# The order of the three passes of an output projection in a two-layer hybrid decoder trunk

## The chip, the core and the metric

The kernel runs on one core of one Trainium2 chip. The metric is the device time of one execution in microseconds (us). The kernel before takes 1791.77 us, the median of three runs (1791.28 to 1794.01). PE is TensorE, DVE is VectorE, ACT is ScalarE, POOL is GpSimd and SP is SyncE, which issues most of the loads.

## What is computed

The input is 512 tokens of width 1024 in float32. Each of the two layers is a feed-forward block, a mixer, and a second feed-forward block. The mixer has two groups of 512 channels each, and one output projection for both:

```python
x = x + 0.5 * swiglu(rms_norm(x, ffn1_norm[l]), ...)
h = rms_norm(x, mix_norm[l])
a, g, q, k, v = jnp.split(h @ w_in[l], splits, axis=-1)
conv_out = conv_module(a, g, conv_w[l], conv_b[l], conv_norm[l])
...
diff_out = diff_attention(q, k, v, rel_bias, lam, lam_init, subln_norm[l])
x = x + jnp.concatenate([conv_out, diff_out], axis=-1) @ w_out[l]
x = x + 0.5 * swiglu(rms_norm(x, ffn2_norm[l]), ...)
```

The conv group is a gated linear unit, a causal depthwise convolution of 31 taps, an RMS norm over the channels and a swish. The attention group is causal: for each of 4 heads, two softmax maps over the same values, of which one is taken from the other with a factor; queries are swept in 4 blocks of 128.

## The kernel before

**Layout.** Activations lie with features on the partitions: `x` is 8 tiles of 128 features by 512 tokens. Every product that matters is made in three matmuls (`mm3`, lines 199, 202, 203): both operands are split into a rounded part and a remainder (`whi`, `wlo` for weights; `acth`, `actl` for activations), and hi by hi, hi by lo and lo by hi are summed in PSUM.

**Weights.** `chunk` (lines 104 to 110) loads 128 rows by 1024 columns in two pieces of 512 columns on SP's queue (line 108) into `wraw`, and `parts_of` splits each: ACT copies it to `whi` (line 100), and DVE or POOL takes the difference to `wlo` (line 101). For the output projection the difference is made by POOL (the argument `G`). These tiles come from rings: 5 buffers of `wraw`, 9 of `whi` and 9 of `wlo`. A buffer is filled again when its last reader is done. One piece of the output weights serves one column block of 128 outputs (`wpart`): 4 tiles of the contraction by 128 columns.

**Order of the work.** The program is written as one stream. A scheduler sorts it at compile time into a fixed queue for each engine: it simulates the time at which each instruction becomes ready and, among the ready ones, prefers those written earlier. At run time each engine works its queue in order and waits on semaphores. Some instructions are held in program order by hand (in the feed-forward blocks); those of the output projection are not.

**The mixer** (`mixer`). After the input projections, `attend` (line 972 on) runs 16 steps, query block 3 first and block 0 last, four heads each. A step makes two score matmuls (line 908) into banks of the tags "sc" and "po", adds the bias and takes a minimum on DVE (line 912), the exponential on ACT (line 916), combines the two maps on DVE (line 922), transposes the map (line 929, copy by ACT in line 931) and multiplies with the values (line 938). After the fourth head of a block, its output is normed (lines 945 to 953), transposed (line 965) and split into `acth` and `actl`, feature tiles 4 to 7, for its 128 tokens (lines 967 and 968). The convolution's taps run on DVE (line 877) and POOL beside it; `conv_finish` then norms the four channel tiles (line 888 on POOL), takes the swish (line 890 on ACT, line 891 on DVE) and writes the split result to `acth` and `actl`, feature tiles 0 to 3 (lines 892 on ACT and 893 on DVE).

**The output projection** is the last part of the mixer. It goes over three pairs of a group and a range of tokens: the conv group (`half` 0) for all 512 tokens, then the attention group (`half` 1) for tokens 256 to 511, then the attention group for tokens 0 to 255. Each pass makes 8 column blocks of 12 matmuls into banks that alternate between the tags "sc" and "po" (two banks each), and DVE adds each block to `x` (line 1016). The list `w` holds the split weights; it is emptied at the start of the first two passes, so the third uses the tiles of the second. In the third pass, and behind it, `after` prepares the next feed-forward block's input (lines 291 to 300) for each finished tile of `x`.

**Behind it** comes the second feed-forward block (`begin`, `ffn`), whose first weights use the same rings and the same SP queue.

Of the kernel before, what the change touches and what calls it, by code (L numbers as in the profile page):

```python
# [20 lines left out]
SEQ = 512  # L21
# [48 lines left out]
def trunk(ctx: ExitStack, tc: tile.TileContext, xt, par, lamv, relb, onehot,  # L70
# [17 lines left out]
    def bank(tag, name):  # L88
        return psum.tile([P, 512], F32, tag=tag, name=name, bufs=BANKS[tag])
# [14 lines left out]
    def chunk(src, eng=None):  # L104
        w = []
        for n in range(2):
            raw = ring("wraw")
            nc.sync.dma_start(raw, src[:, n * 512 : (n + 1) * 512])
            w.append(parts_of(raw, eng))
        return w  # L110

    def wpart(w, b, n=P):
        hi, lo = w[b * n // 512]
        c = b * n % 512
        return hi[:, c : c + n], lo[:, c : c + n]
# [81 lines left out]
    def mm3(ps, w, x, start, stop, pin=False):  # L197
        (wh, wl), (xh, xl) = w, x
        first = T.matmul(ps, wh, xh, start=start, stop=False)  # L199
        if pin:  # L200
            tc.keep_in_program_order(first)
        T.matmul(ps, wh, xl, start=False, stop=False)  # L202
        T.matmul(ps, wl, xh, start=False, stop=stop)  # L203
# [532 lines left out]
    def mixer(l, pr, after, begun):  # L736
        with tc.tile_pool(name="mix", bufs=1) as mp, tc.tile_pool(name="mt", bufs=2) as mt:
# [265 lines left out]

            for half, t in ((0, slice(0, SEQ)), (1, slice(SEQ // 2, SEQ)), (1, slice(0, SEQ // 2))):
                if t.stop == SEQ:
                    w = [None] * 4
                for m in range(KT):
                    if w[m // 2] is None:  # L1010
                        w[m // 2] = chunk(wout[l, half, m // 2], G)
                    ps = bank(("sc", "po")[m % 2], "ps_out")[:, : t.stop - t.start]
                    for kk in range(4):
                        k = half * 4 + kk
                        mm3(ps, wpart(w[m // 2], (m % 2) * 4 + kk), (ch[:, k, t], cl[:, k, t]), kk == 0, kk == 3)
                    V.tensor_tensor(x[:, m, t], ps, x[:, m, t], op=ALU.add)

                    if half == 1 and t.start == 0 and m < KT // 2:
                        after(m)
# [14 lines left out]
    for l in range(DEPTH):  # L1034
        nxt = {}

        def preparing(gain, l2=l):
            def after(m):
                if m == 0:
                    nxt["p"] = Prep(l2, gain)  # L1040
                nxt["p"].tile(m)
            return after

        def store(m):
            nc.sync.dma_start(out[m], x[:, m, :])

        with tc.tile_pool(name="ffn", bufs=1) as fp:
            begun = ffn(fp, pr, gu1[l], dn1[l], preparing("mix_norm"), begun,
                        lambda tail: begin(nxt["p"], [[wag[l, c, i] for i in range(2)] for c in range(2)], tail),
                        (l == 0, 1), aside if l == 0 else None)  # L1050
        mixer(l, nxt["p"], preparing("ffn2_norm"), begun)
        with tc.tile_pool(name="ffn", bufs=1) as fp:
            begun = begin(nxt["p"], [[gu2[l, m, i] for i in range(2)] for m in range(2)])
            if l + 1 < DEPTH:
                begun = ffn(fp, nxt["p"], gu2[l], dn2[l], preparing("ffn1_norm", l + 1), begun,
                            lambda tail: begin(nxt["p"], [[gu1[l + 1, m, i] for i in range(2)] for m in range(2)], tail), (0, 1))
            else:
                ffn(fp, nxt["p"], gu2[l], dn2[l], store, begun, lambda tail: tail(), (0, 0))
        pr = nxt["p"]
# [74 lines left out]
```

## Time and profile before

| | |
|---|---|
| median of three runs | 1791.77 us |
| the profiled execution | 1792.68 us |
| its span, first to last instruction | 1790.9 us |
| mean granted clock of PE | 0.995 |
| output projection, layer 0: first and last matmul start | 506.22 and 554.78 us |
| output projection, layer 1: first and last matmul start | 1394.26 and 1442.32 us |
| loads of output weights | 32, of 256 KB |

A line of the timeline gives the start, the length from the first start to the last end, the engine, the line of the kernel, the operation, what it writes and reads, and the count of merged instructions. What stands in square brackets is the idle time of the engine just before, and what ended it. Matmuls overlap in the pipeline, so the spacing of their starts tells their rate, not their length. The granted clock is the share of full speed that PE's clock was given.

### The profile page before, as it was taken

The numbers are of one execution on the slowest core, as the hardware profiler recorded it, in microseconds if no ns is written. First come the engines' busy times: TensorE is split into PE (matmuls) and PEld (weight loads), VectorE is DVE, ScalarE is ACT, GpSimd is POOL, SyncE is SP. The second block draws the span as 40 slices with busy tenths as digits, with TensorE's granted clock in tenths as the row PEclk, the third lists the DMA queues.
The fourth block names the chain that finished last, engine by engine and source line by source line (L and its number), as shares of the span: only waits on it lengthen the run. The fifth ranks groups of instructions, "written<-read, shape, count | busy, mean of one in ns | idle before, by whom it ended". The sixth has DMA issues, their size and how long they took to land.

```text
span 1790.9 us, 32884 instructions
## 1 busy us (share of the span) xinstructions
PE 1767.7 (99%) x11844; PEld 1623.8 (91%) x11844; DVE 1475.3 (82%) x2595; ACT 1028.0 (57%) x1930; POOL 555.0 (31%) x523
## 2 busy tenths in 40 slices
PE   8999999999989999999999999999999999999998
PEld 7799999988778889999988999999887888999998
DVE  7969888968867959889987798889688488698887
ACT  5546566655844536556644565666559354465664
POOL 3011112379842011112310121123898320111121
PEclk9999999999999999999999999999999999999999
DMA  6457677533112447677543577766231134476775
GB/s 220 133 137 188 171 197 169 152 107 101 59 48 89 124 124 183 170 190 184 141 143 105 150 177 185 190 162 172 80 100 48 48 107 132 130 186 160 202 177 124
DMA packets 163012, 253.58 MB, mean 142 GB/s; under 512 B 18871, under 2 KB 60614, under 8 KB 162848
## 3 DMA queue, kind: packets, MB, share of 16 engines
q1 hardware_dynamic: 126144, 197.19, 34.2%
q0 software_dynamic: 36416, 54.12, 18.5%
q8 instruction: 93, 1.52, 0.3%
q14 instruction: 71, 0.58, 0.1%
q10 hardware_dynamic: 288, 0.16, 0.0%
HBM read 249.28 MB, written 3.42 MB: 141 GB/s over the span
## 4 chain that ended last, share of the span: by engine, by line
PE 90%; DVE 4%; ACT 4%; DMA 1%; issue 1%; POOL 1%; SPq 0%; ACTq 0%; DVEq 0%; POOLq 0%
PE ps_pair L413 36%; PE ps_pair L502 14%; PE ps_pair L202 9%; PE ps_pair L199 9%; PE ps_pair L203 9%; PE ps_out L199 2%; PE ps_out L202 2%; PE ps_out L203 2%; PE ps_pair L793 2%; PE ps_pair L792 2%; PE ps_pair L791 2%; ACT whi L100 1%; DMA wraw<-in_dn 1%; PE ps_v L821 0%; PE ps_sc L908 0%
## 5 line engine op out<-in xcount | busy, mean ns | idle before, releaser
L100 ACT ACTIVATE whi<-wraw 128x512 fp32r<-128x512 f32 x736 | 447.2, 627 | 419.0 <-PE ps_pair L202 163.1
L101 DVE TENSOR_TENSOR wlo<-wraw,whi 128x512 fp32r<-128x512 f32 x648 | 440.1, 698 | 108.8 <-ACT whi L100 93.5
L159 POOL DMA_DIRECT2D wsum<-in_gu x128 | 112.3, 914 | 708.6 <-DMA wsum<-in_gu 308.7
L413 PE MATMUL ps_pair<-acth,wlo 128*128 128x256 f32 x1024 | 289.8, 283 | 0.0
L413 PE MATMUL ps_pair<-actl,whi 128*128 128x256 f32 x1024 | 289.8, 283 | 0.0
L413 PE MATMUL ps_pair<-acth,whi 128*128 128x256 f32 x1024 | 289.8, 283 | 0.0
L413 PE MATMUL ps_pair<-th,whi 128*128 128x256 f32 x768 | 217.3, 283 | 0.0
L413 PE MATMUL ps_pair<-tl,whi 128*128 128x256 f32 x768 | 217.3, 283 | 0.0
L413 PE MATMUL ps_pair<-th,wlo 128*128 128x256 f32 x768 | 217.3, 283 | 0.0
L199 PE MATMUL ps_pair<-acth,whi 128*128 128x512 f32 x512 | 200.2, 395 | 5.6 <-ACT whi L100 5.6
L202 PE MATMUL ps_pair<-actl,whi 128*128 128x512 f32 x512 | 200.3, 392 | 0.0
L203 PE MATMUL ps_pair<-acth,wlo 128*128 128x512 f32 x512 | 199.5, 391 | 0.0
L413 PEld LDWEIGHTS ps_pair<-actl,whi 128*128 128x128 f32 x1024 | 196.6, 192 | 0.2
L413 PEld LDWEIGHTS ps_pair<-acth,whi 128*128 128x128 f32 x1024 | 196.6, 192 | 0.2
L413 PEld LDWEIGHTS ps_pair<-acth,wlo 128*128 128x128 f32 x1024 | 196.6, 192 | 0.0
L159 POOL DMA_DIRECT2D wsum<-in_dn x112 | 98.9, 1137 | 269.6 <-DVE wlo L101 49.9
L413 PEld LDWEIGHTS ps_pair<-th,whi 128*128 128x128 f32 x768 | 147.5, 192 | 0.0
L413 PEld LDWEIGHTS ps_pair<-tl,whi 128*128 128x128 f32 x768 | 147.5, 192 | 0.0
L413 PEld LDWEIGHTS ps_pair<-th,wlo 128*128 128x128 f32 x768 | 147.5, 192 | 0.0
L101 DVE TENSOR_TENSOR wlo<-wsum,whi 128x512 fp32r<-128x512 f32 x192 | 130.4, 685 | 20.2 <-ACT whi L100 16.3
L502 PE MATMUL ps_pair<-hh,whi 128*128 128x256 f32 x512 | 144.9, 283 | 0.0
L502 PE MATMUL ps_pair<-hl,whi 128*128 128x256 f32 x512 | 144.9, 283 | 0.0
(201 smaller groups left out, 4481.0 us busy)
## 6 DMA issues: line engine op xcount, KB each, us to landing
wraw<-in_gu SPq DMA_DIRECT2D x288, 256.0 KB, 3.4
wsum<-in_gu SPq DMA_DIRECT2D x128, 256.0 KB, 3.8
wsum<-in_gu POOLq DMA_DIRECT2D x128, 256.0 KB, 4.7
wraw<-in_dn SPq DMA_DIRECT2D x68, 256.0 KB, 3.1
wraw<-in_wqkv SPq DMA_DIRECT2D x48, 256.0 KB, 2.7
wraw<-in_dn SPq DMA_DIRECT2D x64, 128.0 KB, 3.3
wraw<-in_wag SPq DMA_DIRECT2D x32, 256.0 KB, 2.8
wraw<-in_wout SPq DMA_DIRECT2D x32, 256.0 KB, 2.7
```

Of the source, the lines that this page charges most:

```text
L100: S.activation(hi, raw, AF.Copy)
L101: (eng or V).tensor_tensor(out=lo, in0=raw, in1=f32(hi), op=ALU.subtract)
L159: nc.gpsimd.dma_start(dst[:, to], src, accum_op=ALU.add)
L199: first = T.matmul(ps, wh, xh, start=start, stop=False)
L202: T.matmul(ps, wh, xl, start=False, stop=False)
L203: T.matmul(ps, wl, xh, start=False, stop=stop)
L413: mm = T.matmul(ps, l, r, start=first and i == j == 0, stop=False, skip_group_check=True)
L502: mm = T.matmul(ps, s[:, f], r, start=side not in self.begun, stop=False, skip_group_check=True)
L791: T.matmul(ps[n], xh[:, t], wh, start=k == 0, stop=False)
L792: T.matmul(ps[n], xh[:, t], wl, start=False, stop=False)
L793: T.matmul(ps[n], xl[:, t], wh, start=False, stop=k == KT - 1)
```

## The change

```diff
-            for half, t in ((0, slice(0, SEQ)), (1, slice(SEQ // 2, SEQ)), (1, slice(0, SEQ // 2))):
-                if t.stop == SEQ:
-                    w = [None] * 4
+            for half, t in ((1, slice(SEQ // 2, SEQ)), (0, slice(0, SEQ)), (1, slice(0, SEQ // 2))):
+                w = [None] * 4
                 for m in range(KT):
                     if w[m // 2] is None:
                         w[m // 2] = chunk(wout[l, half, m // 2], G)
```

The attention group for tokens 256 to 511 is taken first, the conv group second, the attention group for tokens 0 to 255 third, as before. The list of weights is emptied at the start of every pass. The conv group lies between the two attention passes, so the attention weights are loaded and split twice: 24 pieces per layer where there were 16. Matmuls, their shapes, the banks' tags and the additions to `x` stay as many as they were. The weights of the first attention pass take the place of the conv weights at the head of the loads, and the conv weights follow them.

## The prediction

> **What bounds the kernel now.** I read the page first: the busy line, and the shares of the chain that ended last.
>
> ```profile
> PE 1767.7 (99%) x11844; PEld 1623.8 (91%) x11844; DVE 1475.3 (82%) x2595; ACT 1028.0 (57%) x1930; POOL 555.0 (31%) x523
> PE 90%; DVE 4%; ACT 4%; DMA 1%; issue 1%; POOL 1%; SPq 0%; ACTq 0%; DVEq 0%; POOLq 0%
> ```
>
> PE is busy for 1767.7 of 1790.9 us and makes 90% of the chain. The change leaves the matmuls as many as they are, so it can win only time in which PE idles or runs slowly. I then read PE's timeline where the output projection begins, in layer 0 and in layer 1.
>
> ```profile
> 490.16 0.60 PE L965 MATMUL ps_o<-ident,ov 128*128 128x128 f32 x4
> 490.59 0.83 PE L938 MATMUL ps_o<-vv,at 128*128 128x128 f32 x6
> ...
> 501.58 0.49 PE L908 MATMUL ps_sc<-kt,qz 128*128 128x128 f32 x2 [0.79 <-DVE e L922]
> ...
> 502.55 0.33 PE L929 MATMUL ps_at<-ident,e 128*128 128x128 f32 x1 [0.37 <-DVE mn L912]
> ...
> 503.88 0.49 PE L938 MATMUL ps_o<-vv,at 128*128 128x128 f32 x2 [0.78 <-ACT at L931]
> ...
> 506.22 2.08 PE L199 MATMUL ps_out<-acth,whi 128*128 128x512 f32 x4 [1.75 <-ACT acth L892]
> ...
> 520.53 0.39 PE L202 MATMUL ps_out<-actl,whi 128*128 128x512 f32 x1
> 520.76 0.39 PE L203 MATMUL ps_out<-acth,wlo 128*128 128x512 f32 x1
> ...
> 531.87 0.28 PE L199 MATMUL ps_out<-acth,whi 128*128 128x256 f32 x1
> ```
>
> ```profile
> 1389.62 0.49 PE L908 MATMUL ps_sc<-kt,qz 128*128 128x128 f32 x2 [0.80 <-DVE e L922]
> ...
> 1390.59 0.33 PE L929 MATMUL ps_at<-ident,e 128*128 128x128 f32 x1 [0.37 <-DVE mn L912]
> ...
> 1391.92 0.49 PE L938 MATMUL ps_o<-vv,at 128*128 128x128 f32 x2 [0.78 <-ACT at L931]
> ...
> 1392.98 0.79 PE L938 MATMUL ps_o<-vv,at 128*128 128x128 f32 x2 [0.43 <-ACT at L931]
> 1394.26 2.07 PE L199 MATMUL ps_out<-acth,whi 128*128 128x512 f32 x4 [0.48 <-ACT acth L892]
> ```
>
> The brackets are PE's idle time: 0.79 + 0.37 + 0.78 + 1.75 = 3.69 us in layer 0 and 0.80 + 0.37 + 0.78 + 0.43 + 0.48 = 2.86 us in layer 1. From one 512-wide matmul to the next it is 0.23 us (520.53 to 520.76; from 520.53 to 531.87 there are 50, 0.227 us each), and the 192 256-wide ones run from 531.87 to 554.90 (last fence of this part), 0.12 us each. Four 128-wide ones take from 490.16 to 490.59, 0.11 us each. The first matmuls of the projection are slower, and the windows say why (columns: window, its length, PE busy and instructions, granted clock, DMA share, GB/s).
>
> ```profile
> 506.22:511.83 5.61, 5.61 (x14) 0.51 0.00 0
> 1394.26:1399.38 5.12, 5.12 (x12) 0.52 0.00 0
> ```
>
> PE is busy throughout, at half the clock. In layer 0 these are twelve 512-wide and two 128-wide matmuls, at full clock 12 x 0.227 + 2 x 0.11 = 2.95 us, so 2.66 us are lost; in layer 1 5.12 - 2.73 = 2.39 us. All that can be won here is 3.69 + 2.66 = **6.35 us** and 2.86 + 2.39 = **5.25 us**, together 11.6 us.
>
> **The change part by part.** *The attention group of tokens 256 to 511 goes first* (96 matmuls, 96 x 0.12 = 11.5 us, which I call the first pass). Its operands and banks, on DVE:
>
> ```profile
> 499.13 0.28 DVE L912 CUSTOM_DVE_ANT_0 e<-ps_sc,bias 128x128 f32<-128x128 f32 x1
> ...
> 499.34 0.74 DVE L968 SCALAR_TENSOR_TENSOR actl<-ps_o,gsub,acth 128x512 fp32r<-128x512 f32 x1
> ...
> 501.94 0.35 DVE L922 SCALAR_TENSOR_TENSOR e<-ps_sc,c,e 128x128 f32<-128x128 f32 x1
> ...
> 503.86 1.56 DVE L891 SCALAR_TENSOR_TENSOR yp<-th,yp 128x512 f32<-128x512 f32 x1
> ...
> 506.87 0.68 DVE L891 SCALAR_TENSOR_TENSOR u<-th,u 128x512 f32<-128x512 f32 x1
> ...
> 512.85 0.74 DVE L893 SCALAR_TENSOR_TENSOR actl<-u,ghalf,acth 128x512 fp32r<-128x512 f32 x1
> ```
>
> L968 at 499.34 writes the split output of query block 2; block 3 came before it. So the operands stand at 500.08. The projection takes its banks from the tags "sc" and "po", which the maps still use: the last map leaves "sc" after L912 at 499.41, the one before it leaves "po" after L922 at 502.29. The first pass can start at about 500.2 with column blocks 0 and 2 (12 x 0.12 = 1.44 us each), and block 1 waits for 502.29. If PE takes strictly 0, 1, 2, it waits from about 501.9, 0.4 us. So I leave 0 to 0.4 us per layer in place, and take 0.4.
>
> Blocks 1 and 0 still write acth and actl, in stripes of the same tile between those that the pass reads. That such a write doesn't hold up the reader is seen elsewhere:
>
> ```profile
> 193.25 0.28 PE L502 MATMUL ps_pair<-yl,whi 128*128 128x256 f32 x1
> ```
>
> ```profile
> 193.44 0.95 DVE L473 TENSOR_TENSOR yl<-ht,yh 128x768 fp32r<-128x768 f32 x1
> ```
>
> PE reads other stripes of yl before DVE's write, earlier in the program, has begun.
>
> *The conv group becomes second.* Its chain (L891, L892, L893 for four channel tiles) ends at 513.59 now. PE's work from 500.2 on is 11.5 us of first pass and the rest of the attention (L908, L929, L938, L965, some 21 128-wide ones, 2.3 us); with the 0.4 us it reaches the conv group at about 514.4. DVE gets the first pass's eight additions inside the chain's stretch (groups of 515 to 545 us, then windows with PE, weight load, DVE, ACT, POOL busy and the clock):
>
> ```profile
> L101 POOL TENSOR_TENSOR wlo<-wraw,whi 128x512 fp32r<-128x512 f32 x7 | 8.9, 1294 | 10.0 <-ACT whi L100 10.0
> ...
> L1016 DVE TENSOR_TENSOR x<-ps_out,x 128x256 f32<-128x256 f32 x8 | 3.4, 425 | 7.2 <-PE ps_out L203 7.1
> ```
>
> ```profile
> 504.90:508.30 3.40, 2.08 (x5) 1.70 (x6) 2.31 (x4) 2.21 (x5) 2.92 (x2) 0.50 0.00 0
> 508.30:511.70 3.40, 3.40 (x10) 2.72 (x10) 3.21 (x6) 2.44 (x5) 1.14 (x2) 0.50 0.00 0
> ```
>
> The eight additions are 3.4 us, and DVE idles 1.09 + 0.19 = 1.28 us in these windows, so the chain ends some 2.1 us later, at 515.7. With three of four channel tiles there, PE has nine matmuls (2.0 us, to 516.4) on one column block, or 36 (8.2 us) if the queue interleaves four blocks, as it does now (x4 at 506.22). So the wait lies between nothing and 3.7 us per layer (worked out under the rivals). I take 1.0, near the lower end, for the row at 506.22.
>
> *The weights.* 24 loads per layer take the place of 16: the second attention pass loads its own again. Seven of now sixteen pieces are split after 515 (the row of POOL above), so nine early, up to the size of the ring:
>
> ```profile
> 478.63 2.51 POOL L101 TENSOR_TENSOR wlo<-wraw,whi 128x512 fp32r<-128x512 f32 x2
> ...
> 502.72 3.64 POOL L888 TENSOR_TENSOR u<-u,rb 128x512 f32<-128x512 f32 x3
> ...
> 510.76 1.45 POOL L243 TENSOR_TENSOR rs_y<-so,mhalf 128x4 f32<-128x4 f32 x1
> ```
>
> ```profile
> 520.96 0.64 ACT L100 ACTIVATE whi<-wraw 128x512 fp32r<-128x512 f32 x1 [0.28 <-PE ps_out L202]
> ```
>
> After the change the early nine are all eight of the first pass and one of the conv group. The other seven conv pieces follow as the first pass frees slots (as ACT at 520.96 waits for a matmul): one per 1.44 us, ACT 0.63, POOL 1.29 us. At worst POOL begins them at 512.2, after L243, and has them ready at 513.5 + 1.3k; the conv group needs piece k at 514.4 + 2.72k. Nothing is late, and POOL is the cover. The eight new pieces of the last pass (ACT 8 x 0.63 = 5.0, POOL 8 x 1.29 = 10.3 us per layer) are split during the conv group's 21.8 us, in which each column block frees one slot; eight of nine slots hold them when the last pass starts. Cost nothing; without that cover each would cost 1.9 us.
>
> ```profile
> 592.39 0.92 POOL L159 DMA_DIRECT2D wsum<-in_gu  x1 [23.07 <-DMA wsum<-in_gu]
> ```
>
> ```profile
> SPq L108 <- POOL wlo L101: 93.8, 24, 39.2
> ```
>
> ```profile
> wraw<-in_wout SPq DMA_DIRECT2D x32, 256.0 KB, 2.7
> ```
>
> POOL's next own transfer is issued at 592.39, long behind the added splits. The loads' queue waits for buffers (24 waits, 93.8 us from 430 to 560), not the reverse; a load lands in 2.7 us. Behind the eight added loads stand FFN2's first weights, on the same queue. Their slots come free with the last pass, as now, and their raw buffers when pieces 3 to 7 of it are split, before it starts. Cost nothing; the bound is one landing, 2.7 us per layer.
>
> *What is late next.* The last pass and FFN2 follow without a gap now, and PE waits 0.3 us in the 345 us behind:
>
> ```profile
> 554.78 0.28 PE L203 MATMUL ps_out<-acth,wlo 128*128 128x256 f32 x1
> 554.90 0.40 PE L199 MATMUL ps_pair<-acth,whi 128*128 128x512 f32 x1
> ```
>
> ```profile
> PE ps_pair L502 <- ACT keep L535: 0.3, 1, 0.3
> ```
>
> So what is won is kept. **Sum:** 11.6 - 2 x (0.4 + 1.0) = 8.8 us. The profiled execution took 1792.68 us (span 1790.9 and 1.8 around it), which gives 1783.9; it stands 0.9 above the median 1791.77, which gives **1783**.
>
> **The rivals.** *The conv chain comes late.* L891 took 1.56 us at 503.86 and 0.68 at 506.87; in the first case POOL's L888 (from 502.72) ran beside it. The POOL splits that now stand beside five of the chain's instructions could stretch each by the difference of these rows, up to 0.88 us: 4.4 us, and the chain ends at 515.7 + 4.4 = 520.1. PE then stands from 516.4 to 520.1, 3.7 us, if the blocks aren't interleaved: 11.6 - 2 x (0.4 + 3.7) = 3.4, **1788**; half the stretch gives 1.5 us, 7.8, 1784. Of the Trainium skill, the page "SBUF — State Buffer", section "Who interferes with whom", says that a DVE instruction with two SBUF inputs and a GpSimd instruction that reads SBUF exclude one another; by it this rival holds, and the pair of L891 rows agrees.
>
> *The clock falls all the same.* The longest wait was 1.75 us (0.80 in layer 1) and the clock fell in both layers. If filling the gaps doesn't hold it up, 2.66 + 2.39 us stay lost: 8.8 - 5.05 = 3.75, **1788**. The rows speak for the gaps: the clock is full in the uninterrupted matmuls behind. Of the Trainium skill, "TensorE: Matmul & The Clock Gate", section "Why this matters for your kernels", counts only PE-idle gaps of over about 3 us as bringing the slow clock; by it the drop here has another cause and would stay, and the trace's 1.75 us speaks against that figure.
>
> *The pass doesn't start early.* The order on each engine is fixed before the run; if the first pass is queued behind the last map's matmuls and L938, it starts at 506 and again at half clock: nothing won, **1792**.
>
> *Slower: the queues of ACT and DVE put the chain behind the first pass.* The splits on ACT wait for PE to free a slot, the additions on DVE wait for a matmul. If they are queued ahead of L890 to L893, the chain (503.86 to 513.59, 9.7 us) starts only when the pass ends. PE then idles 9.7 us and restarts at half clock (2.66): 12.4 against 6.35 to win, 6 us lost per layer, **1804**. It decides from the point where the last channel tile comes later than 514.4 + 6.35 = 520.7. Against it: the chain is earlier in the program, and DVE and ACT idle between its steps now.
>
> **How the numbers follow.** Forecast 1783 (own range 1780 to 1785): 0.58. Late chain, 1784 to 1788: 0.12, a quarter of it beyond the bound. Clock, 1788: 0.06, half of it beyond. No early start, 1792: 0.08. Slower, 1796 to 1804: 0.16. A measurement of this kernel can tell about 0.2%, 3.6 us, from no change: faster is below 1788.2, slower above 1795.4. Faster 0.58 + 0.09 + 0.03 = 0.70, same 0.03 + 0.03 + 0.08 = 0.14, slower 0.16. The range runs from 1779, the whole 11.6 us and one for the spread, to 1793, with the cases of no gain; it leaves out the slower case and little more.
>
> **What would show it.** First L199 on ps_out with 128x256 at about 500.2 (1388.2), and no wait over 0.5 us before the first 512-wide one at about 514; granted clock 1.00 in windows from 502 to 515; the last 128x256 ending some 4 to 5 us earlier against the start of the projection's stretch; L100 on wout 48 times. Wrong would be: waits on L892 or L893 after 514, clock 0.5 there, or the first ps_out at 506.

## The result, and the profile after

The changed kernel takes **1780.16 us**, the median of six runs (1778.98 to 1780.86), against 1791.97 (1791.28 to 1794.01, six runs) for the kernel before: a ratio of 0.9931, with a 95% interval of 0.9918 to 0.9944. The forecast was 1783, in a range of 1779 to 1793, with faster at 0.70. The profiled executions are 13.7 us apart (1792.68 and 1778.98), the medians 11.8: the one before stands 0.7 us above its median, the one after 1.2 below.

From the page after, the busy line, the chain that ended last, and the loads of output weights:

```profile
span 1777.2 us, 32962 instructions
...
PE 1760.0 (99%) x11844; PEld 1619.0 (91%) x11844; DVE 1478.7 (83%) x2595; ACT 1037.6 (58%) x1946; POOL 579.7 (33%) x539
...
PE 90%; ACT 3%; DVE 3%; DMA 2%; issue 1%; POOL 1%; SPq 0%; ACTq 0%; DVEq 0%; POOLq 0%
...
wraw<-in_wout SPq DMA_DIRECT2D x48, 256.0 KB, 2.6
```

PE has the same 11844 matmuls, and is busy 7.7 us less, although nothing was taken from it: a busy PE at half clock counts as busy (in the prediction's window from 506.22 us it is busy for all 5.61 us at 0.51), and so does the end of a matmul that nothing follows at once (see the idle time below). POOL has 24.7 us more of work (the 16 more splits) and ACT 9.6; neither shows in the time. That POOL's share rose from 31% to 33% tells nothing of whether that work lies on the path.

PE's timeline after, in layer 0, and its last line from layer 1:

```profile
498.79 0.39 PE L199 MATMUL ps_out<-acth,whi 128*128 128x256 f32 x1
...
500.92 0.36 PE L202 MATMUL ps_out<-actl,whi 128*128 128x256 f32 x1
...
503.63 0.39 PE L908 MATMUL ps_sc<-kt,qz 128*128 128x128 f32 x2
503.86 0.27 PE L929 MATMUL ps_at<-ident,e 128*128 128x128 f32 x1
503.88 0.36 PE L199 MATMUL ps_out<-acth,whi 128*128 128x256 f32 x1
...
508.59 0.51 PE L199 MATMUL ps_out<-acth,whi 128*128 128x512 f32 x2
508.94 0.28 PE L202 MATMUL ps_out<-actl,whi 128*128 128x256 f32 x1
...
547.71 0.40 PE L199 MATMUL ps_pair<-acth,whi 128*128 128x512 f32 x1
...
1428.34 0.40 PE L199 MATMUL ps_pair<-acth,whi 128*128 128x512 f32 x1
```

The short attention matmuls (L908, L929) that stood alone before, each behind an idle time, now stand between 256-wide matmuls without a bracket. At 508.59 the first 512-wide matmul of the conv group is already in the queue, between blocks of the first pass: the scheduler mixed the two passes. FFN2's first matmul starts at 547.71, where it started at 554.90, and in layer 1 at 1428.34.

PE's granted clock in four windows after (the third number from the end):

```profile
501.70:505.10 3.40, 3.40 (x31) 3.40 (x30) 2.39 (x9) 2.51 (x6) 3.40 (x4) 1.00 0.00 0
505.10:508.50 3.40, 3.40 (x31) 3.40 (x31) 3.14 (x8) 2.76 (x6) 3.40 (x3) 1.00 0.00 0
508.50:511.90 3.40, 3.40 (x30) 3.27 (x29) 3.06 (x4) 1.81 (x4) 3.40 (x4) 1.00 0.21 62
511.90:515.30 3.40, 3.40 (x27) 3.18 (x26) 2.94 (x4) 2.94 (x5) 3.40 (x3) 1.00 0.48 156
```

PE is busy through all four, at full clock, where it had 0.51 before.

**One length for all kernels below.** I measure the end of the mixer from the row sums of the conv norm (line 250, started before the stretch in question) to FFN2's first matmul. In the timeline of the kernel before, PE:

```profile
494.32 0.60 PE L250 MATMUL ps_rows<-ident,csum 128*128 128x128 f32 x4
...
1382.36 0.60 PE L250 MATMUL ps_rows<-ident,csum 128*128 128x128 f32 x4
...
1442.44 0.40 PE L199 MATMUL ps_pair<-acth,whi 128*128 128x512 f32 x1
```

and in that of the kernel after:

```profile
494.58 0.60 PE L250 MATMUL ps_rows<-ident,csum 128*128 128x128 f32 x4
...
1375.22 0.60 PE L250 MATMUL ps_rows<-ident,csum 128*128 128x128 f32 x4
```

I call this length the **step**. Before: 554.90 - 494.32 = 60.58 us in layer 0 and 1442.44 - 1382.36 = 60.08 in layer 1. After: 53.13 and 53.12. The gain is 7.45 + 6.96 = **14.4 us**. Outside the steps 0.7 us are given back (0.26 before layer 0's, 0.05 between the two, 0.4 behind layer 1's), which leaves the 13.7 of the two spans. So the whole effect lies in these two stretches.

### The profile page after: what moved, and what is told of

Read it like the earlier page. It is cut to its first block, busy times and chain, and to the rows that moved or that the text cites. A ratio compares the mean times of both kernels' runs of the same rounds, so it can differ in the third digit from the quotient of the medians.

```text
span 1777.2 us, 32962 instructions
## 1 busy us (share of the span) xinstructions
PE 1760.0 (99%) x11844; PEld 1619.0 (91%) x11844; DVE 1478.7 (83%) x2595; ACT 1037.6 (58%) x1946; POOL 579.7 (33%) x539
## 4 chain that ended last, share of the span: by engine, by line
PE 90%; ACT 3%; DVE 3%; DMA 2%; issue 1%; POOL 1%; SPq 0%; ACTq 0%; DVEq 0%; POOLq 0%
PE ps_pair L413 36%; PE ps_pair L502 14%; PE ps_pair L202 9%; PE ps_pair L203 9%; PE ps_pair L199 9%; PE ps_out L199 2%; PE ps_out L202 2%; PE ps_out L203 2%; PE ps_pair L793 2%; PE ps_pair L792 2%; PE ps_pair L791 2%; DMA wraw<-in_dn 1%; ACT whi L100 1%; PE ps_sc L908 0%; DVE actl L292 0%
## 5 line engine op out<-in xcount | busy, mean ns | idle before, releaser
L100 ACT ACTIVATE whi<-wraw 128x512 fp32r<-128x512 f32 x752 | 457.4, 627 | 406.8 <-PE ps_pair L202 160.5
L101 POOL TENSOR_TENSOR wlo<-wraw,whi 128x512 fp32r<-128x512 f32 x104 | 137.1, 1339 | 26.4 <-ACT whi L100 20.5
```

The source lines that it names most:

```text
L100: S.activation(hi, raw, AF.Copy)
L101: (eng or V).tensor_tensor(out=lo, in0=raw, in1=f32(hi), op=ALU.subtract)
```

## The experiments

**Theory A** (mine): the early pass gives PE work while the last attention blocks and the conv chain finish; that fills PE's idle time, and since PE no longer idles the clock isn't lowered. Rivals: the gain comes from the order or the second loading of the weights (**B**); the clock falls for a reason of its own; the conv chain, drawn out by POOL, takes part of the gain back. Each kernel was run beside the kernel before, whose median was 1792.89 beside the first eight and 1792.74 beside the last two.

### The second loading alone, in the old order

```diff
-            for half, t in ((1, slice(SEQ // 2, SEQ)), (0, slice(0, SEQ)), (1, slice(0, SEQ // 2))):
+            for half, t in ((0, slice(0, SEQ)), (1, slice(SEQ // 2, SEQ)), (1, slice(0, SEQ // 2))):
```

(against the changed kernel, so that `w = [None] * 4` stays)

> The old order of the passes, but the weights are loaded and split anew in every pass: 24 pieces per layer as in the changed kernel. Theory A (the gain is time in which PE stood still or ran at half clock before the conv group; the second loading is hidden): the time of before, 1792 within 2 us, granted clock 0.5 again in the 5 to 6 us behind the first ps_out matmul. Theory B (the gain comes from the buffers, which come free earlier when the weights aren't held through two passes): 1780 to 1786. If the second loading costs something that the changed kernel had to win back: 1794 to 1797.

Measured: 1792.63 us, ratio 1.0 (0.9991 to 1.0009), with 48 loads. The 8 loads, 8 ACT copies and 8 POOL splits per layer cost nothing, and win nothing: theory B falls.

### The new order in layer 0 alone

```diff
+            up, conv, low = (1, slice(SEQ // 2, SEQ)), (0, slice(0, SEQ)), (1, slice(0, SEQ // 2))
+            for half, t in (up, conv, low) if l == 0 else (conv, up, low):
+                if l == 0 or t.stop == SEQ:
                     w = [None] * 4
```

> The new order in layer 0 only. Theory A: the two layers' stretches are separate, layer 0 gives 7.4 us by the two traces (the step from the 490th us to the first FFN2 matmul), so 1784.5 to 1786 against 1792; layer 1's stretch as before, clock 0.5 there. If the gain is a better schedule of the whole program: nothing like half, 1780 or 1790.

Measured: 1786.25 us, ratio 0.9964 (0.9951 to 0.9976), 0.25 us above the expected span, beside a kernel before that took 0.9 us more here than in the runs of the result. The step is 53.13 us in layer 0 and 60.40 in layer 1: the gain is half, and belongs to the layer that is changed.

### The old order with useless matmuls in the gap

```diff
             conv_finish()
+            idle = bank("y", "ps_idle")[:, : SEQ // 2]
+            for n in range(28):
+                k = CT + n % CT
+                T.matmul(idle, ones_r, ch[:, k, SEQ // 2 :], start=n == 0, stop=n == 27)
```

The 28 matmuls go to a bank that nobody reads; the rest is the kernel before.

> The old order, and 28 matmuls per layer of 128x256 into a bank that nobody reads, in the gap before the conv group (28 x 0.12 = 3.4 us of work that serves nothing). They leave the waits for the conv chain where they are and only keep PE active. Theory A with the clock following PE's idleness: granted clock 1.00 behind the first ps_out matmul, 2.66 + 2.39 = 5.0 us less than before, 1787. Theory C (the clock falls for another reason): clock 0.5, 1792 or up to 2 us more.

Measured: 1787.84 us, ratio 0.9975 (0.9965 to 0.9984), steps of 58.20 and 58.17. This is the kernel before with more work to do, and it is faster. PE's waits from 480 to 560 us (line, what it waited for, us in total, times, longest), and its windows:

```profile
PE ps_o L938 <- ACT at L931: 0.8, 2, 0.5
PE ps_idle L1007 <- ACT rb L278: 0.6, 1, 0.6
PE ps_out L199 <- ACT acth L892: 0.3, 1, 0.3
PE ps_sc L908 <- DVE e L922: 0.3, 1, 0.3
```

```profile
501.70:505.10 3.40, 2.76 (x21) 2.55 (x21) 2.00 (x10) 1.86 (x6) 2.29 (x3) 1.00 0.02 5
505.10:508.50 3.40, 3.40 (x25) 3.13 (x24) 2.81 (x5) 2.02 (x6) 3.40 (x4) 1.00 0.00 0
508.50:511.90 3.40, 3.07 (x16) 2.36 (x15) 3.10 (x7) 1.78 (x4) 1.32 (x1) 1.00 0.00 0
511.90:515.30 3.40, 3.40 (x20) 2.83 (x19) 1.84 (x3) 2.38 (x5) 0.00 (x0) 1.00 0.00 0
```

The clock is 1.00 throughout, with the conv group, its weights and its chain where they were: the half clock followed PE's idleness and nothing else that the change touches. The useless matmuls (28 x 0.12 = 3.4 us per layer) stand roughly for the idle time that they fill (PE's waits in the stretch shown fall from 4.8 to 2.0 us), so what is left as gain is the clock: 5.05 us by the medians, 2.38 + 1.91 = 4.3 by the steps, where the prediction had 2.66 + 2.39. The rule that the prediction weighed, of the Trainium skill, "TensorE: Matmul & The Clock Gate", section "Why this matters for your kernels" (of gaps that bring the slow clock back, it names PE-idle ones of over about 3 us), does not agree as a limit: in the kernel before no gap was longer than 1.75 us in layer 0 and 0.80 us in layer 1, and the clock was halved in both.

### Only two column blocks first

```diff
+            up, conv, low = slice(SEQ // 2, SEQ), slice(0, SEQ), slice(0, SEQ // 2)
+            for half, t, ms in ((1, up, range(2)), (0, conv, range(KT)), (1, up, range(2, KT)), (1, low, range(KT))):
                 w = [None] * 4
-                for m in range(KT):
+                for m in ms:
```

> Only two of the eight column blocks of tokens 256 to 511 go first (2 x 1.44 = 2.9 us of PE work), the other six behind the conv group. Theory A: 2.9 of some 4.5 us of each layer's standing time are filled, 5.8 us in both layers; with the clock kept up 5.0 more, 1781; with the clock falling all the same, 1786. PE waits for the conv chain again (L892 or L893 as releaser), 1 to 2 us per layer. If order alone or the buffers made the gain: 1780 without such waits.

Measured: 1782.93 us, ratio 0.9951 (0.9939 to 0.9964), steps of 55.52 and 55.49, clock 1.00. A quarter of the early work (2.9 of 11.5 us) brings 5.06 of layer 0's 7.45 us. The clock is won first; what remains is idle time. The time is 2 us above the expected 1781, and the wait for the conv chain is smaller than expected, 0.2 us per layer (L893); the other waits of this stretch (2.2 us from 480 to 560 us) are for the maps of the attention.

### The blocks of the first two passes kept in program order

```diff
                         mm3(ps, wpart(w[m // 2], (m % 2) * 4 + kk), (ch[:, k, t], cl[:, k, t]), kk == 0, kk == 3,
+                            pin=t.stop == SEQ)
```

> The changed kernel, but the matmuls of the first two passes are kept in program order: column block after column block, no mixing of four blocks or of the two passes. The conv chain ends at 517.4 in the changed kernel. Theory A (the mixing of blocks hides the late chain): PE waits 0.4 us for a bank of the tag po in the first pass and about 1.0 us per layer for L892 or L893 in the conv group, 1783 (this is the sum of the prediction with its two reserves). If the mixing does nothing: 1780.

Measured: 1783.94 us, ratio 0.9958 (0.9946 to 0.997), steps of 55.58 in both layers. The changed kernel itself, run again beside it:

> The changed kernel once more, to stand beside the next three on the same chip: 1780 within 1.5 us.

Measured: 1779.33 us (five runs), ratio 0.9926 (0.9913 to 0.9939), steps of 53.12 and 53.13. PE's waits from 480 to 560 us with the blocks in order:

```profile
PE ps_o L938 <- ACT at L931: 1.3, 3, 0.5
PE ps_out L202 <- DVE actl L893: 1.0, 1, 1.0
PE ps_sc L908 <- DVE e L922: 0.3, 1, 0.3
```

and those of the changed kernel, in the same window:

```profile
PE ps_o L938 <- ACT at L931: 0.8, 2, 0.5
PE ps_sc L908 <- DVE e L922: 0.3, 1, 0.3
```

With the blocks in order PE waits 1.0 us for the conv chain's last result (L893) and 0.5 us more for the maps that stand between the blocks. Free to mix, it has neither wait: the mixing is worth 55.58 - 53.13 = 2.45 us per layer, and the late chain is real but covered. The waits make up 1.5 of the 2.45 us; the rest was not taken apart. The expected wait of 0.4 us for a bank did not come.

### The conv weights split by DVE instead of POOL

```diff
-                        w[m // 2] = chunk(wout[l, half, m // 2], G)
+                        w[m // 2] = chunk(wout[l, half, m // 2], V if half == 0 else G)
```

> The changed kernel, but the conv group's eight weight pieces are split by DVE and not by POOL. The two L891 that took 1.78 us beside POOL's splits should take 0.7 us, and the conv chain loses about 2 us of length but shares DVE with eight splits of 0.69 us. Theory A (the chain has cover): 1780 within 2 us, however the chain ends. If POOL's splits beside DVE cost time in the changed kernel: 1776 to 1778.

Measured: 1790.51 us, from 1782.93 to 1797.05 over twelve runs, ratio 0.9987 (0.9973 to 1.0). This missed by 10 us: the gain is gone. The loss begins long before the projection. DVE's, POOL's and PE's timelines in the profiled execution of this kernel:

```profile
477.25 5.33 DVE L101 TENSOR_TENSOR wlo<-wraw,whi 128x512 fp32r<-128x512 f32 x1 [0.32 <-POOL wlo L101]
```

```profile
475.86 2.51 POOL L101 TENSOR_TENSOR wlo<-wraw,whi 128x512 fp32r<-128x512 f32 x2
478.33 1.27 POOL L863 TENSOR_TENSOR yp<-yp,prod 128x512 f32<-128x512 f32 x1
479.55 1.26 POOL L101 TENSOR_TENSOR wlo<-wraw,whi 128x512 fp32r<-128x512 f32 x1
480.77 1.26 POOL L863 TENSOR_TENSOR yp<-yp,prod 128x512 f32<-128x512 f32 x1
```

```profile
484.15 2.50 PE L908 MATMUL ps_sc<-kt,qz 128*128 128x384 f32 x4 [4.23 <-DVE e L922]
```

One split, which takes DVE 0.68 us when it is alone (513.41 in the next kernel), took 5.33 us: it ends at 482.58, 0.55 us after POOL's unbroken run of five instructions (480.77 + 1.26 = 482.03). DVE's map work (L922) stands in the queue behind it, and PE idles 4.23 us for that. Behind the stop PE's clock is halved, long before the projection:

```profile
484.15:488.00 3.85, 3.85 (x12) 2.96 (x13) 2.32 (x8) 2.62 (x7) 1.27 (x1) 0.50 0.52 173
```

The steps of this kernel are 56.78 and 56.81 us, with two waits of PE for DVE in layer 0, 0.7 us (an addition) and 0.5 us (L953); what makes up the 3.7 us more than in the changed kernel, the delay ahead of them or DVE's other splits, the next kernel separates in part. The trace is that of one execution, of 1793.4 us. Over the twelve the mean granted clock goes with the time, from 1.000 in the fastest to 0.996 in the slowest; whether the stop is absent in the fast ones no trace shows.

### The same, but the first piece stays on POOL

```diff
+                        w[m // 2] = chunk(wout[l, half, m // 2], V if half == 0 and m else G)
```

> The changed order, with the conv projection's pieces split by DVE instead of POOL, except the first piece (row blocks 0 and 1), which stays on POOL. Theory S (the one DVE split at 477 us that took 5.33 us beside an unbroken run of POOL, and the 4.2 us that PE waited behind it at 484 us, are all that the version with every conv split on DVE lost): no wait of 4 us on PE ahead of the projection, steps from the row sums to the next feed-forward of about 53.1 us in both layers, 1780 us (1778 to 1782). Theory T (DVE's splits beside the conv chain cost by themselves, because they delay the scores' and the chain's own DVE work): 1784 to 1790, with PE waiting for DVE inside the projection and steps of 55 to 57 us.

Measured: **1777.95 us** (1777.85 to 1779.54), ratio 0.992 (0.9906 to 0.9933), steps of 53.17 and 53.16. Theory S holds: with the two splits of the first piece on POOL, the first DVE split of the stretch comes at 505 us, and the eleven from there to 547 us (six for the conv group, five that the changed kernel has too) add nothing to the step. One of them in DVE's timeline:

```profile
513.41 0.68 DVE L101 TENSOR_TENSOR wlo<-wraw,whi 128x512 fp32r<-128x512 f32 x1
```

### The other half of the tokens first

```diff
+            for half, t in ((1, slice(0, SEQ // 2)), (0, slice(0, SEQ)), (1, slice(SEQ // 2, SEQ))):
...
-                    if half == 1 and t.start == 0 and m < KT // 2:
+                    if half == 1 and t.start and m < KT // 2:
```

> The same three passes, but tokens 0 to 255 take the first place and tokens 256 to 511 the last; the query blocks still run from 3 to 0, so what goes first is ready last (block 0, 514 to 520 us now). Theory A (what counts is that the first pass's operands are there at 500): PE stands until about 514 with little to do (one conv piece is split early), 3 to 5 us worse per layer than before, 1797 to 1803. If having an attention pass ahead of the conv group is what helps, whichever: 1780 to 1786.

Measured: 1808.02 us, ratio 1.0085 (1.0072 to 1.0098), steps of 67.40 and 67.10. The direction is as expected, the size 5 us more. PE's waits from 480 to 560 us (the two longest), and two of its windows:

```profile
PE ps_o L938 <- ACT at L931: 4.1, 4, 2.5
PE ps_o L965 <- ACT acth L892: 3.5, 1, 3.5
```

```profile
508.50:511.90 3.40, 1.16 (x5) 0.72 (x4) 3.23 (x6) 3.06 (x6) 0.66 (x3) 0.50 0.00 0
511.90:515.30 3.40, 1.09 (x4) 0.72 (x4) 2.69 (x5) 1.42 (x3) 0.61 (x1) 0.50 0.00 0
```

Tokens 0 to 255 are the blocks that the attention finishes last, so this first pass has nothing to do early, and the conv group waits behind it. "Attention first" is not what helps: the pass whose operands are ready is. The second row of the waits names the conv chain's copy on ACT (L892), which ended at 513.99 us. But the attention's output that L965 transposes (written by DVE in L953) stood only at 513.84, so without that copy PE would have waited nearly as long for block 0's own norm. I had counted the wait of the first pass alone; how the 5 us divide was not taken apart.

### Half of the early work, the rest at full width

```diff
+            up, conv, low = slice(SEQ // 2, SEQ), slice(0, SEQ), slice(0, SEQ // 2)
+            for half, t, ms in ((1, up, range(4)), (0, conv, range(KT)), (1, conv, range(4, KT)), (1, low, range(4))):
                 w = [None] * 4
-                for m in range(KT):
+                for m in ms:
...
-                    if half == 1 and t.start == 0 and m < KT // 2:
+                    if half == 1 and t is low:
```

> Tokens 256 to 511 of the attention group come first for row blocks 0 to 3 only, then the conv group for all blocks, then the attention group: blocks 4 to 7 at the full 512 tokens in one matmul each, blocks 0 to 3 for tokens 0 to 255. It has 48 matmuls of 128x512 and 96 of 128x256 fewer per layer than two halves would need, worth 48 x (2 x 0.12 - 0.227) = about 0.6 us per layer, and four piece loads fewer. Theory A (5.8 us of early work are enough to cover the late conv chain, since two blocks, 2.9 us, left only about 2.4 us of waits per layer): no new waits, steps of about 52.5 us instead of 53.13, 1778.5 to 1780. Rival (four blocks don't cover the chain): PE waits for the conv chain's last result, the step is 53.5 us or more and the time 1780.5 to 1782.

Measured: 1778.06 us (1777.22 to 1778.18), ratio 0.9917 (0.9903 to 0.993), steps of 53.49 and 53.50. The time falls within theory A's span but the step does not: it isn't 52.5 us. There is a wait that the changed kernel doesn't have, in the timeline of PE:

```profile
506.27 0.85 PE L199 MATMUL ps_out<-acth,whi 128*128 128x512 f32 x3 [0.63 <-ACT acth L892]
```

These 0.63 us take back what the 48 saved matmuls give; the other 0.3 us of the miss I didn't take apart. The time stands level with that of the DVE splits (1777.95, same chip), and the intervals of both ratios overlap that of the changed kernel (0.9913 to 0.9939 when run again), so neither is shown to be faster. Four blocks instead of eight are almost enough.

## Why the prediction was right, and where its terms were off

**PE is the bound, and only idle and slow time can be won.** Right. The gain lies in the two steps, with as many matmuls as before.

**Half clock, 2.66 + 2.39 us.** Right, and shown by the useless matmuls, with 5.05 us by the medians and 4.3 by the steps. The rival that the clock falls all the same is out.

**Idle time, 3.69 + 2.86 us.** This term was mis-sized. The brackets count from the end of one matmul to the start of the next. In an unbroken row the next matmul starts before the one ahead has ended; before a stop the whole length of the last one passes, and the brackets leave that out. In the kernel before, PE's timeline:

```profile
500.40 0.38 PE L938 MATMUL ps_o<-vv,at 128*128 128x128 f32 x2
...
504.20 0.27 PE L929 MATMUL ps_at<-ident,e 128*128 128x128 f32 x1
...
1388.44 0.38 PE L938 MATMUL ps_o<-vv,at 128*128 128x128 f32 x2
```

Two matmuls take 0.38 us and a lone one 0.27, against 0.11 us each from start to start in an unbroken row. From 500.40 to 506.22 there are 5.82 us and eleven 128-wide matmuls, 1.2 us of work: 4.6 us are lost, not 3.69. In layer 1, 1388.44 to 1394.26 is 5.82 us with thirteen, 1.43 us: 4.4, not 2.86. With the clock that makes 4.6 + 2.66 = 7.3 and 4.4 + 2.39 = 6.8 us, against gains of 7.45 and 6.96. So the "all that can be won" of 11.6 us was no upper bound. Counted from start to start it is some 14.1 us, and 0.3 of the 14.4 stay unaccounted for.

**The two reserves, 0.4 for the bank and 1.0 for the late chain per layer.** Both were nothing in the changed kernel. A wait for L893 of 1.0 us appears once the blocks are kept in order, but that it meets the reserve is luck: the prediction chose 1.0 between nothing and 3.7 us, for a chain that ends at 515.7 and a PE that reaches the conv group at 514.4, and in that kernel the two are 519.25 and 515.49. Mixing the blocks, which the prediction named as one possibility (36 matmuls to cover with instead of nine), is what removed it. The bank's 0.4 didn't appear as a wait by itself in any run; the one wait of `ps_out` for DVE to free a bank, 0.7 us behind an addition, stands where DVE makes all the conv splits.

**The conv chain ends at 515.7, with 520.1 as the bound.** It ended between them. DVE's and POOL's timelines after:

```profile
507.25 0.69 DVE L891 SCALAR_TENSOR_TENSOR u<-th,u 128x512 f32<-128x512 f32 x1
...
510.55 1.78 DVE L891 SCALAR_TENSOR_TENSOR u<-th,u 128x512 f32<-128x512 f32 x1
...
513.95 1.78 DVE L891 SCALAR_TENSOR_TENSOR u<-th,u 128x512 f32<-128x512 f32 x1
...
516.64 0.79 DVE L893 SCALAR_TENSOR_TENSOR actl<-u,ghalf,acth 128x512 fp32r<-128x512 f32 x1
```

```profile
508.78 12.31 POOL L101 TENSOR_TENSOR wlo<-wraw,whi 128x512 fp32r<-128x512 f32 x8
```

L891 takes 0.69 us ahead of POOL's eight splits and 1.78 us beside them. The mechanism of the rival "the conv chain comes late" was there, 1.1 us twice, and the chain ended at 517.4, not 515.7. The rival's bound of 0.88 us for each of five instructions was wrong both ways: the three L893 beside the splits took 0.79 to 0.91 us, against 0.74 alone. The late chain cost nothing, since PE had other blocks to do. The rule of the Trainium skill, "SBUF — State Buffer", section "Who interferes with whom" (a DVE instruction with two SBUF inputs and a GpSimd instruction that reads SBUF exclude one another), agrees with the rows of L891. The L893, which have two SBUF inputs as well, lost little here; with the blocks in order two of them took 1.30 and 1.80 us.

**The early start at 500.2 and 1388.2.** Right in kind: single matmuls of the pass stand at 498.79 already, 1.4 us earlier than forecast (they read `acth` alone, and the forecast waited for `actl`), and it runs without a stop from 500.92. In layer 1 everything lies 7 us sooner, by what layer 0 gave. The first 512-wide matmul came at 508.59, not at 514, because of the mixing. **48 loads at no cost.** Right, by the second loading alone. **The slower rival** (the chain queued behind the first pass) didn't happen: DVE took L891 and L893 between the additions. Its mechanism, a queue that stands behind one instruction, shows where DVE makes all the conv splits, at 477 us.

**The sum.** 11.6 - 2.8 = 8.8 us was forecast; 14.1 - 0 is what the corrected terms give, 14.4 was measured in the steps and 13.7 in the spans. The medians, 11.8 apart, ended 2.8 us below the 1783. That the miss is 2.8 us and not 13.7 - 8.8 = 4.9 is luck: the two profiled executions, of which the first gave the terms, stand further apart than the medians. That 11.8 is close to the 11.6 is luck too.

## What to carry to other kernels

When an engine that sets the end idles in short stops, look for work whose operands are already there and put it ahead of what is late; here a quarter of it, 2.9 us, won two thirds of the gain, because it also kept the clock up. Count what the stops cost from start to start, against the rate of an unbroken row, since the idle brackets leave out the end of each lone matmul. And leave the scheduler blocks to mix: here the late chain cost nothing, because another block could be taken.

## What was unexpected of the hardware

- A DVE instruction beside POOL can wait for several POOL instructions: a split of 0.68 us took 5.33 us, to the end of an unbroken run of POOL. At other times it gets in between them: L891 took 1.78 us beside the eight splits of the changed kernel, less than one split of 12.31 / 8 = 1.54 us and its own 0.69 together. What decides between the two the runs do not show, nor why the times of that kernel scatter over 14 us. That the first piece's splits are the cause was shown by leaving them, and them alone, on POOL (the scheduler sorted the queues anew, so their order can differ elsewhere too).
- Short gaps were enough to halve the clock. In windows of 0.2 us of the kernel before, it fell at 504.9 us in layer 0, 0.4 us into the gap of 1.75 us, and at 1392.3 us in layer 1, after gaps of 0.80, 0.37 and 0.78 us, 1.95 us of idle time within 3.5 us. It stayed at 1.00 with waits of at most 0.6 us, 2.0 us in total from 480 to 560 us (useless matmuls), and with 2.6 us in total of at most 1.0 us in the same window (blocks in order).
- How long the half clock lasts varies. In the kernel with the second loading alone, PE's waits in layer 0 are those of the kernel before, to 0.1 us. Two windows of that kernel, then the same two of the kernel before:

```profile
505.10:508.50 3.40, 1.66 (x7) 1.17 (x8) 2.61 (x3) 1.50 (x3) 3.40 (x3) 0.90 0.00 0
508.50:511.90 3.40, 3.40 (x12) 2.79 (x11) 2.90 (x6) 2.79 (x5) 0.66 (x3) 0.60 0.00 0
```

```profile
505.10:508.50 3.40, 2.28 (x7) 1.90 (x7) 2.31 (x5) 2.41 (x5) 2.72 (x2) 0.50 0.00 0
508.50:511.90 3.40, 3.40 (x11) 2.68 (x10) 3.21 (x6) 2.24 (x4) 1.34 (x2) 0.53 0.00 0
```

In windows of 0.2 us the half clock lasts from 507.8 to 511.2 us with the second loading and from 504.9 to 511.7 before; in layer 1 from 1395.3 to 1398.7 and from 1392.3 to 1399.2. That is 3.4 us in both layers of the one and 6.8 us in both of the other. What sets the length the runs do not show. The step in layer 0 was 59.65 us with the second loading, against 60.58 before.
